# A PSUM bank for the preparation of two recurrences, an earlier place for the second group's start, and a drain that steps only its own heads, in a hybrid decoder layer

## The chip, the core and the metric

The kernel runs on one core of one Trainium2 chip. The metric is the device time of one launch in microseconds (us); it is given as the median of several runs. TensorE (PE) does the matrix multiplications and writes to PSUM, VectorE (DVE) and ScalarE (ACT) do elementwise work, GpSimd (POOL) a few small operations, and SyncE (SP) issues the DMAs that bring in the weights.

## The reference

One decoder layer on x of 256 positions by 2048 channels, all in float32:

```python
x = layer_norm(alpha * x + 0.5 * swiglu(x, ffn1_w_gate, ffn1_w_up, ffn1_w_down), ln1_g, ln1_b)
p = x @ w_in                                     # columns of both mixers
o_attn = diff_attn_group(p[..., :ATTN_COLS], ...)   # 8 heads, two softmaxes each, ALiBi, causal
o_rwkv = rwkv7_group(p[..., ATTN_COLS:], ...)       # 16 heads of 64, delta-rule state over time
mix = jnp.concatenate([o_attn, o_rwkv], axis=-1) @ w_out
x = layer_norm(alpha * x + mix, ln2_g, ln2_b)
x = layer_norm(alpha * x + 0.5 * swiglu(x, ffn2_w_gate, ffn2_w_up, ffn2_w_down), ln3_g, ln3_b)
```

The recurrence of a head carries a 64 by 64 state over the 256 positions, with a decay, a key, a value and a rate for every position:

```python
sa = einsum('bhvk,bhk->bhv', state, -kk_t)
state = state * w_t + sa[..., None] * (kk_t * a_t) + v_t[..., None] * k_t
y_t = einsum('bhvk,bhk->bhv', state, r_t)
```

## The kernel before

**Main stream.** Every large product goes through `Stream.block` (L119). It takes two rows of 128 of the weight matrix at a time by 512 columns: SP loads them into `raw` (three buffers), ACT rounds them to `wh` (L137), DVE takes the rest as `wl` (L138), and PE multiplies three times, high by high, low by high, high by low (L113 to L115). Each step of a block gives 6 such large matmuls for the first 128 positions and 6 for the second 128, the latter two steps behind in the mixer (`LAG`). The mixer has five buffers each for `wh` and `wl`.

**The mixer's side work.** The mixer lies between the two feed-forward parts. Its side work is written as Python generators that are spawned into the stream. After each step, `run_bg` (L154) lets every generator go on by as much as its credit allows (1.6 units a step for the recurrences, 0.5 for the attention heads). A `drain` emits steps until given generators have ended; before the change it goes round all live generators, one step each (L168 to L180). What the generators emit is the order in which the program is recorded; a scheduler then places the instructions of each engine by a timeline of its own, so an instruction may stand some way from where it was recorded.

**What is in a recurrence.** There are two groups of eight recurrent heads, r1 (g = 0) and r2 (g = 1), and two groups of four attention heads, a1 and a2. `rwkv_cols` makes the columns of a group (three blocks of w_in) and spawns `rwkv_group` (L483) and `rwkv_values` (L456). `rwkv_group` has a preparation and a chain. The preparation: rates and decays from two small products (L496, L497, sigmoids at L500, L501), the running sum (L505), the norm of the keys (L519, L520), eight elementwise steps of 128 by 1024 on DVE (L524 to L545), and the products of all pairs within a chunk (L555, masked at L558). Then a triangular system is solved on DVE in 31 steps (L583, L585), the result goes through DRAM and back (L589 to L601, issued by ACT), and two small products complete it (L608, L619), with transposes at L629. The chain goes over four chunks c of 64 positions, each a sequence of PE steps of eight small matmuls with a DVE or ACT step behind each: L642, L650, L658, then L675 and L681 for the output. The tail of a group: centring (L696, L697), squares (L700), L706, Ln and Exp (L707, L709), scale and shift (L711, L714, L716), and the gate (L727, L730, L731). L81 and L82 split the group's output for the product with w_out.

**An attention head** (`attn_heads`, L760) is a chain over all engines too: logits L774, L776, maximum L779, Exp L784, normalisation L786 to L790, transposes L795, product with the values L801 to L803, root mean square L811 to L825, and transposes L829. Two heads of a group go at the same time.

**PSUM.** The eight banks are: three for the large matmuls' `acc`, two with the tag "at" (transposes and attention), and three with the tag "sm" for all small products of the recurrences.

**The order of the mixer** stands at L839 to L890: columns of r1, a1, r2; drain of a1's heads; columns of a2; then the output projection in three parts, for a1 and r1 together (`parts` entry (0, 2)), for a2, and for r2. Each part first drains the generators that make its input (`ready`, L847). So the last part of the projection needs the end of r2's tail, and the part before it needs the end of a2's heads.

Of the kernel before, what the change touches and what calls it, by code (L numbers as in the profile page):

```python
# [12 lines left out]
AF = mybir.ActivationFunctionType  # L13
# [3 lines left out]
P = 128  # L17
D = 2048
S = 256
# [11 lines left out]
LAG = {"ffn": 4, "mix": 2}  # L31
NW = {"ffn": 7, "mix": 5}
NRAW = 3
BANKS = {"tr": ("at", 2), "sm": ("sm", 3), "at": ("at", 2)}
BG = 1.6
AT = 0.5

# [1 line left out]
def build(tc, A, out):  # L39
# [19 lines left out]
    V, SC, G, T = nc.vector, nc.scalar, nc.gpsimd, nc.tensor  # L59
# [29 lines left out]
    class Stream:  # L89
# [75 lines left out]
                        break  # L165
                    c[0] -= cost

        def until(self, ready):  # L168
            idle = 0
            while not ready():  # L170
                assert idle < len(self.bg)
                g = self.bg.pop(0)
                try:
                    idle = idle + 1 if next(g) is None else 0
                    self.bg.append(g)
                except StopIteration:
                    pass

        def drain(self, gens):
            self.until(lambda: not any(g in self.bg for g in gens))  # L180

    stream = Stream()
    KX = [(k, k) for k in range(16)]
# [146 lines left out]
    def mix(mp, pq, C):  # L330
        vB, om = C["vB"], C["om"]

        def bank(tag, shape=(P, NB)):
            return pq.tile(list(shape), F32, tag=BANKS[tag][0], name=nm(tag), bufs=BANKS[tag][1])

        w_in = A["w_in"][0]
        R0 = 3 * AW
        lora = {}
# [73 lines left out]
                self.tl = hp.tile([P, 4, S], F32, tag=HT["T2"], name=nm("tl")) if g == 0 else mp.tile([P, 4, S], F32, tag="tl", name=nm("tl"))  # L412
                self.cum = hp.tile([P, 4, S], F32, tag=HT["T1"], name=nm("cum")) if g == 0 else qq[:, 1]

        def rwkv_cols(g, prev=None):
            gr = Group(g)
            st = {"prev": prev, "group": gr}
            if prev is not None:
                prev["next"] = st
            st["gen"] = rwkv_group(g, st)  # L420
            stream.spawn(st["gen"], BG)

            def done(tt, acc, i):
# [17 lines left out]
            return st  # L441

        def col(i, g, p):
            k = 24 + 8 * i + 4 * g + p
            return vB[:, k:k + 1]
# [10 lines left out]
        def rwkv_values(g, st):  # L456
            prev = st["prev"]
            while "rk" not in st or (prev is not None and "chain" not in prev):
                yield None
            vp, vv, rk = st["group"].vp, st["group"].vv, st["rk"]  # L460
            SV = hp.tile([P, 4, 4, 2, 64], F32, tag="J1", name=nm("SV"))
            st["SV"] = SV
            for p in range(4):
                ps = bank("sm", (P, 4, P))
                for c in range(4):
                    T.transpose(ps[:, c, :], vp[:, p, c * 64:c * 64 + P], ident)
                SC.copy(out=SV[64:128, p, :, 0, :], in_=ps[64:128, :, 0:64])
                SC.copy(out=SV[0:64, p, 0:3, 1, :], in_=ps[0:64, 1:4, 64:128])
                yield 0.3
            ps = bank("sm", (P, 4, P))  # L470
            for p in range(4):
                T.transpose(ps[0:64, p, :], vv[:, p, 192:256], ident)
            SC.copy(out=SV[0:64, :, 3, 1, :], in_=ps[0:64, :, 64:128])
            yield 0.3
            for hf in range(2):
                ps = bank("sm", (P, 2, S))
                for p in range(2):
                    T.matmul(ps[:, p, :], C["bones"], rk[:, 2 * hf + p, :], start=True, stop=True)
                V.tensor_tensor(out=vv[:, 2 * hf:2 * hf + 2, :], in0=ps, in1=vv[:, 2 * hf:2 * hf + 2, :], op=ALU.mult)
                yield 0.6  # L480
            st["values"] = True

        def rwkv_group(g, st):  # L483
            prev, gr = st["prev"], st["group"]
            AR, BK, vv, al, rh, be, ka, av, tl, cum = gr.AR, gr.BK, gr.vv, gr.al, gr.rh, gr.be, gr.ka, gr.av, gr.tl, gr.cum
            wa = cum.rearrange("p a s -> p (a s)")[:, 0:NB]
# [2 lines left out]
            while "tw" not in lora:  # L489
                yield None  # L490
            for hf in range(2):
                pw = bank("sm", (P, 2, S))
                pl = bank("sm", (P, 2, S))
                for i in range(2):
                    c0 = (2 * hf + i) * P
                    T.matmul(pw[:, i, :], wa[0:64, c0:c0 + P], lora["tw"][0:64], start=True, stop=True)  # L496
                    T.matmul(pl[:, i, :], wa[64:128, c0:c0 + P], lora["tw"][64:128], start=True, stop=True)  # L497
                for i in range(2):
                    p = 2 * hf + i
                    SC.activation(out=tl[:, p, :], in_=pw[:, i, :], func=AF.Sigmoid, bias=col(0, g, p))  # L500
                    SC.activation(out=av[:, p], in_=pl[:, i, :].rearrange("p (c t) -> p c t", c=4), func=AF.Sigmoid, bias=col(1, g, p))  # L501
                yield 0.6

            for p in range(4):
                V.tensor_tensor_scan(out=cum[:, p, :], data0=C["smask"], data1=tl[:, p, :], initial=0.0, op0=ALU.mult, op1=ALU.add)  # L505
# [8 lines left out]
                V.tensor_scalar(out=be[:, p], in0=av[:, p], scalar1=-1.0, scalar2=col(3, g, p), op0=ALU.add, op1=ALU.mult)  # L514
            yield 1.0
            for hf in range(2):
                ps = bank("sm", (P, 2, S))
# [30 lines left out]
                yield None  # L548

            for p in range(4):  # L550
                pe = [bank("sm", (P, 4, P)) for e in range(2)]
                for c in range(4):
                    for e in range(2):
                        r = slice(64 * e, 64 * e + 64)
                        T.matmul(pe[e][:, c, :], BK[r, p, c, e:e + 2].rearrange("p a t -> p (a t)"),  # L555
                                 AR[r, p, c].rearrange("p a t -> p (a t)"), start=True, stop=True)
                for e in range(2):
                    V.tensor_tensor(out=Q[:, p, :, e, :], in0=pe[e], in1=C["maskq"][:, None, :].to_broadcast([P, 4, P]), op=ALU.mult)  # L558
                yield 1.2
# [400 lines left out]
```

## Time and profile before

| | |
|---|---|
| three runs | 2024.72, 2017.95, 2019.3 us; median 2019.3 us |
| the profiled execution | 2024.08 us, its span 2022.2 us, clock 0.984 |
| busy in the span | PE 1977.3 us, DVE 1147.5, ACT 883.7, POOL 35.7 |
| the mixer | about 750 to 1290 us of the span |

The profile is that of one execution. Its page gives the busy time of each engine, a chain of work that ended last, and groups of instructions by line. The trace behind it answers by stretches: for a window of time it gives the busy time of each engine and the granted clock of PE (PEclk, 1.00 is full speed); for a wait it gives who waited for whom; and a timeline lists the instructions one by one, with the idle time before each and what ended it in square brackets. A PE busy time says nothing of the rate: at half the clock the same matmuls are busy for twice as long.

### The profile page before, as it was taken

Reading aid. Unit: us, or ns where it says so; the run is one execution under the profiler, and the core shown is the slowest. Engines: PE = TensorE matmul, PEld = TensorE weight load, DVE = VectorE, ACT = ScalarE, POOL = GpSimd, SP = SyncE. Lnnn points to the kernel's source line nnn. Section 1 sums busy time; section 2 is a strip of 40 time slices with the busy share of each in tenths; the row PEclk is TensorE's granted clock in tenths of the full one; section 3 lists DMA queues with packets and bytes.
Section 4 is the critical chain, followed back from the end, with each engine's and each line's share of the span. In section 5 each row is a group of like instructions: output and inputs, shape, how many; then the busy total and the mean of one; then the engine's idle time right before and its main releaser. Section 6 shows DMA issues by size and latency. Waiting matters only on the chain. (4 is left out here: it accounts for less than half of the span.)

```text
span 2022.2 us, 24923 instructions
## 1 busy us (share of the span) xinstructions
PE 1977.3 (98%) x9671; PEld 1623.3 (80%) x9671; DVE 1147.5 (57%) x1419; ACT 883.7 (44%) x1095; POOL 35.7 (2%) x68
## 2 busy tenths in 40 slices
PE   9999999999999999999999988899999999999997
PEld 7888888888888878887777766788888888888886
DVE  5555554445545566775767865755555444555555
ACT  5444433344443335645574443444444334444432
POOL 0200000000000000000000000000000000000000
PEclk9999999999999999999999978999999999999999
DMA  7766666667666656565444624666665666766663
GB/s 243 218 188 195 185 191 209 207 193 229 192 188 188 196 163 196 160 176 163 136 121 141 207 63 154 194 203 187 189 195 185 206 208 198 230 188 189 187 194 129
DMA packets 202009, 373.35 MB, mean 185 GB/s; under 512 B 22827, under 2 KB 24945, under 8 KB 201121
## 3 DMA queue, kind: packets, MB, share of 16 engines
q1 hardware_dynamic: 182928, 350.53, 57.9%
q10 hardware_dynamic: 17440, 14.29, 2.5%
q0 software_dynamic: 1520, 6.93, 1.0%
q8 instruction: 76, 1.25, 0.3%
q14 instruction: 45, 0.36, 0.1%
HBM read 364.10 MB, written 7.60 MB: 184 GB/s over the span
## 5 line engine op out<-in xcount | busy, mean ns | idle before, releaser
L138 DVE TENSOR_TENSOR wl<-raw,wh 128x1024 fp32r<-128x1024 f32 (+1 forms) x665 | 808.0, 1216 | 670.3 <-ACT wh L137 669.3
L137 ACT CAST wh<-raw 128x1024 fp32r<-128x1024 f32 (+1 forms) x665 | 695.4, 1047 | 848.8 <-PE acc L115 733.6
L115 PE MATMUL acc<-wh,xl 128*128 128x512 f32 (+1 forms) x1952 | 741.8, 392 | 0.5 <-DVE xl L82 0.5
L114 PE MATMUL acc<-wl,xh 128*128 128x512 f32 (+1 forms) x1952 | 737.4, 393 | 0.7 <-DVE wl L138 0.7
L113 PE MATMUL acc<-wh,xh 128*128 128x512 f32 (+1 forms) x1952 | 725.5, 392 | 8.5 <-ACT xh L81 5.6
L113 PEld LDWEIGHTS acc<-wh,xh 128*128 128x128 f32 x1952 | 368.9, 189 | 87.5 <-ACT xh L81 7.1
L115 PEld LDWEIGHTS acc<-wh,xl 128*128 128x128 f32 x1952 | 368.9, 189 | 77.2 <-issue 2.0
L114 PEld LDWEIGHTS acc<-wl,xh 128*128 128x128 f32 x1952 | 369.0, 189 | 76.6 <-DVE wl L138 1.8
L115 PE MATMUL acc<-wh,hh 128*128 128x512 f32 x704 | 254.4, 390 | 0.0
L114 PE MATMUL acc<-wl,hh 128*128 128x512 f32 x704 | 253.5, 389 | 0.0
L113 PE MATMUL acc<-wh,hh 128*128 128x512 f32 x704 | 252.8, 389 | 0.0
L114 PEld LDWEIGHTS acc<-wl,hh 128*128 128x128 f32 x704 | 132.2, 188 | 27.6
L113 PEld LDWEIGHTS acc<-wh,hh 128*128 128x128 f32 x704 | 132.1, 188 | 27.4
L115 PEld LDWEIGHTS acc<-wh,hh 128*128 128x128 f32 x704 | 132.2, 188 | 27.3
L243 DVE TENSOR_TENSOR hh<-tr,hh 128x512 fp32r<-128x512 f32 x44 | 30.4, 691 | 64.1 <-ACT hh L242 64.1
L242 ACT CAST hh<-tr 128x512 fp32r<-128x512 f32 x44 | 25.8, 586 | 91.2 <-PE tr L232 91.2
L229 DVE SCALAR_TENSOR_TENSOR h<-sg,acc 128x512 f32<-128x512 f32 x44 | 30.2, 687 | 34.7 <-PE acc L115 34.7
L224 ACT ACTIVATE sg<-acc 128x512 f32<-128x512 f32 x44 | 26.3, 598 | 43.5 <-PE acc L115 43.5
L232 PEld LDWEIGHTS tr<-ident,h 128*128 128x128 f32 x176 | 21.9, 140 | 5.7
L232 PE MATMUL tr<-ident,h 128*128 128x128 f32 x176 | 26.3, 272 | 0.0
L583 DVE TENSOR_TENSOR itmp<-U,Y 64x31 f32<-64x31 f32 (+15 forms) x62 | 20.6, 333 | 4.1 <-DMA U<-dU 2.8
L585 DVE TENSOR_TENSOR Y<-Y,itmp 64x31 f32<-64x31 f32 (+15 forms) x62 | 20.6, 332 | 1.3
(239 smaller groups left out, 753.2 us busy)
## 6 DMA issues: line engine op xcount, KB each, us to landing
raw<-in_ffn_w_up_dram SPq DMA_DIRECT2D x176, 512.0 KB, 3.9
raw<-in_ffn_w_down_dram SPq DMA_DIRECT2D x176, 512.0 KB, 4.3
raw<-in_ffn_w_gate_dram SPq DMA_DIRECT2D x175, 512.0 KB, 3.9
raw<-in_w_in_dram SPq DMA_DIRECT2D x96, 512.0 KB, 3.7
raw<-in_w_out_dram SPq DMA_DIRECT2D x32, 512.0 KB, 4.1
xs<-y ACTq DMA_DIRECT2D x16, 256.0 KB, 3.3
rc<-xs ACTq DMA_DIRECT2D x16, 256.0 KB, 4.4
lng<-in_ln_g_dram POOLq DMA_DIRECT2D x3, 1024.0 KB, 7.8
```

Source lines behind the costliest of these rows:

```text
L113: T.matmul(a, hi, wh[:, j, :w], start=(ki + j == 0), stop=False)
L114: T.matmul(a, hi, wl[:, j, :w], start=False, stop=False)
L115: T.matmul(a, lo, wh[:, j, :w], start=False, stop=(ki + j == last))
L137: SC.copy(out=wh[:, c, :w], in_=raw[:, c, :w])
L138: V.tensor_tensor(out=wl[:, c, :w], in0=raw[:, c, :w], in1=wh[:, c, :w].bitcast(F32), op=ALU.subtract)
L224: SC.activation(out=s, in_=acc, func=AF.Silu)
L229: V.scalar_tensor_tensor(out=h, in0=sg[tt], scalar=0.5, in1=acc, op0=ALU.mult, op1=ALU.mult)
L232: T.transpose(tr[:, i, :], h[:, i * P:(i + 1) * P], ident)
L242: SC.copy(out=hi, in_=tr)
L243: V.tensor_tensor(out=lo, in0=tr, in1=hi.bitcast(F32), op=ALU.subtract)
L583: V.tensor_tensor(out=tv, in0=U[:, 0:j, j:j + 1].to_broadcast([64, j, 32 - j]), in1=Y[:, j:j + 1, j:32].to_broadcast([64, j, 32 - j]), op= ...
L585: V.tensor_tensor(out=Y[:, 0:j, j:32], in0=Y[:, 0:j, j:32], in1=tv, op=ALU.add)
```

## The change

There are three edits, in the mixer alone. No instruction's work changes.

1. PSUM: the tag "sm" has two banks instead of three, and the third gets the tag "pr". The preparation and the values of a group use "pr" (rates, key norms, transposes of the values, bonus products; of the pair products one of each two in every other pair). The rates' two products, which stood in two banks at once, now stand one after the other in the one bank, each with its sigmoids.
2. `rwkv_cols` is split: `rwkv_start` allocates the group's tiles and spawns its generator, `rwkv_cols` makes the columns. The second group is started right behind the first's columns, ahead of a1's.
3. `drain` steps only the generators that it was given; it steps another one only where none of its own can go on.

```diff
-BANKS = {"tr": ("at", 2), "sm": ("sm", 3), "at": ("at", 2)}
+BANKS = {"tr": ("at", 2), "sm": ("sm", 2), "pr": ("pr", 1), "at": ("at", 2)}
...
+        def advance(self, g):
+            try:
+                return next(g) is not None
+            except StopIteration:
+                self.bg.remove(g)
+                return True
 
         def drain(self, gens):
-            self.until(lambda: not any(g in self.bg for g in gens))
+            while any(g in self.bg for g in gens):
+                if not any([self.advance(g) for g in gens if g in self.bg]):
+                    assert any([self.advance(g) for g in self.bg if g not in gens])
...
-        def rwkv_cols(g, prev=None):
+        def rwkv_start(g, prev=None):
...
             for p in range(4):
-                ps = bank("sm", (P, 4, P))
+                ps = bank("pr", (P, 4, P))
                 for c in range(4):
                     T.transpose(ps[:, c, :], vp[:, p, c * 64:c * 64 + P], ident)
...
             for hf in range(2):
-                pw = bank("sm", (P, 2, S))
-                pl = bank("sm", (P, 2, S))
...
+                for k in range(2):
+                    ps = bank("pr", (P, 2, S))
...
             for p in range(4):
-                pe = [bank("sm", (P, 4, P)) for e in range(2)]
+                pe = [bank("sm", (P, 4, P)), bank(("sm", "pr")[p % 2], (P, 4, P))]
...
-        r1 = rwkv_cols(0)
+        r1 = rwkv_start(0)
+        rwkv_cols(0, r1)
+        r2 = rwkv_start(1, r1)
         a1 = attn_cols(0)
-        r2 = rwkv_cols(1, r1)
+        rwkv_cols(1, r2)
         stream.drain(gens(a1))
```

The built programs show what the three edits move. In the pieces below, a line of the mixer in the changed kernel is one higher than the same line before (L609 is L608, L620 is L619, L697 is L696, L707 is L706, L728 is L727). `acc` is a large matmul's output, `wh` and `wl` its weights, `xh` and `xl` its input.

On PE, where the second group's two small products stand that complete its triangular system (L608 writes what becomes PT, L619 uses it). Before (the one large matmul in it is the last that does not need a2's heads):

```order
L608 MATMUL sm_8451<-YT_8447,Q 32x32 x32
L115 MATMUL acc_9640<-wh_9668,xl_9150 128x512
L619 MATMUL sm_8507<-TT_8441,PT_8448 32x32
L629 MATMUL sm_8544<-ident,BK_7242 128x64 x8
L829 MATMUL at_9414<-ident,ot_9319 128x128 x2
L774 MATMUL at_9441<-k_8144,qq 128x128
L774 MATMUL at_9441<-k_8144,qq 128x256
L619 MATMUL sm_8507<-TT_8441,PT_8448 32x32 x31
```

The same place in the changed program:

```order
L609 MATMUL sm_8451<-YT_8447,Q 32x32 x32
L796 MATMUL at_9276<-ident,s_9180 128x128 x3
L113 MATMUL acc_9424<-wh_9462,xh_9137 128x512
...
L115 MATMUL acc_9424<-wh_9528,xl_9146 128x512
L802 MATMUL at_9315<-v_8145,pT_9280 128x128
L620 MATMUL sm_8507<-TT_8441,PT_8448 32x32
L803 MATMUL at_9315<-v_8145,pT_9280 128x128
L804 MATMUL at_9315<-v_8145,pT_9280 128x128
L113 MATMUL acc_9424<-wh_9528,xh_9145 128x512
L620 MATMUL sm_8507<-TT_8441,PT_8448 32x32 x31
L630 MATMUL sm_8544<-ident,BK_6297 128x64 x8
```

One large matmul stood between L608 and the first of L619, and none between it and the others; now 26 stand between the first two, one more before the others, and 57 between those and the stretch without large matmuls that follows. That stretch begins behind the same large matmul in both programs (the 4608th of the whole program), the last that does not need a2's heads. Before, it holds the rest of L619, L629, both heads' logits and the chain's chunks 0 to 2; now it holds chunk 0 from L658 on and chunks 1 to 3, and both heads from L795 on.

On PE, in the second group's tail, between its centring (L696) and the first large matmul that takes its output (`xh_9865`). Before:

```order
L696 MATMUL sm_8890<-BK_7242,bones 128x256 x2
L696 MATMUL sm_8920<-BK_7242,bones 128x256 x2
L115 MATMUL acc_9831<-wh_9846,xl_9697 128x512
L114 MATMUL acc_9838<-wl_9807,xh_9700 128x512
L115 MATMUL acc_9838<-wh_9806,xl_9701 128x512
L706 MATMUL sm_8925<-BK_7242,bones 128x256 x2
L706 MATMUL sm_8929<-BK_7242,bones 128x256 x2
L727 MATMUL sm_8986<-gs_5667,g_1652_8887 128x256 x2
L730 MATMUL sm_8986<-gs_5668,g_1652_8887 128x256 x2
L727 MATMUL sm_9011<-gs_5667,g_1652_8887 128x256 x2
L730 MATMUL sm_9011<-gs_5668,g_1652_8887 128x256 x2
L113 MATMUL acc_9883<-wh_9878,xh_9865 128x512
```

And now:

```order
L697 MATMUL sm_8890<-BK_6297,bones 128x256 x2
L697 MATMUL sm_8920<-BK_6297,bones 128x256 x2
L115 MATMUL acc_9751<-wh_9746,xl_9697 128x512
...
L115 MATMUL acc_9791<-wh_9786,xl_9697 128x512
L707 MATMUL sm_8925<-BK_6297,bones 128x256 x2
L707 MATMUL sm_8929<-BK_6297,bones 128x256 x2
L113 MATMUL acc_9791<-wh_9806,xh_9696 128x512
...
L728 MATMUL sm_8986<-gs_5667,g_1652_8887 128x256 x2
L731 MATMUL sm_8986<-gs_5668,g_1652_8887 128x256 x2
L728 MATMUL sm_9011<-gs_5667,g_1652_8887 128x256 x2
L731 MATMUL sm_9011<-gs_5668,g_1652_8887 128x256 x2
...
L113 MATMUL acc_9883<-wh_9878,xh_9865 128x512
```

Between L696 and L706 there were 3 large matmuls and are now 23; between L706 and L727 none, and now 19; between the last L730 and the first matmul that needs the output none, and now 23.

On DVE, the second group's elementwise preparation (writes to AR and BK) among the weights' casts (`wl`). Before:

```order
L526 TENSOR_TENSOR AR_7241<-AR_7241,tl_7245 128x16x64
L138 TENSOR_TENSOR wl_8741<-raw_8739,wh_8740 128x1024
L531 SCALAR_TENSOR_TENSOR BK_7242<-BK_7242,AR_7241 128x16x64
L367 SCALAR_TENSOR_TENSOR vv_7243<-praw_8116,om,df_8206 128x256
L533 TENSOR_TENSOR BK_7242<-BK_7242,tl_7245 128x16x64
L138 TENSOR_TENSOR wl_8795<-raw_8793,wh_8794 128x1024
L535 TENSOR_TENSOR BK_7242<-BK_7242,tl_7245 64x16x64
L536 TENSOR_TENSOR BK_7242<-BK_7242,tl_7245 64x16x64
L539 COPY PC_7791<-qq 128x16
L540 TENSOR_TENSOR AR_7241<-AR_7241,qq 128x16x63
L545 TENSOR_TENSOR AR_7241<-AR_7241,qq 128x16x64
L138 TENSOR_TENSOR wl_8842<-raw_8840,wh_8841 128x1024
```

And now, from one cast to the next:

```order
L138 TENSOR_TENSOR wl_8275<-raw_8273,wh_8274 128x1024
L823 TENSOR_TENSOR ars_7802<-ars_7802,fl_7801 128x4
L527 TENSOR_TENSOR AR_6296<-AR_6296,tl_6300 128x16x64
L824 TENSOR_TENSOR ars_7802<-ars_7802 128x2
L532 SCALAR_TENSOR_TENSOR BK_6297<-BK_6297,AR_6296 128x16x64
L826 TENSOR_SCALAR ot_7798<-at_7794,ars_7802 128x128 x2
L534 TENSOR_TENSOR BK_6297<-BK_6297,tl_6300 128x16x64
L536 TENSOR_TENSOR BK_6297<-BK_6297,tl_6300 64x16x64
L537 TENSOR_TENSOR BK_6297<-BK_6297,tl_6300 64x16x64
L813 TENSOR_SCALAR ot_7812<-at_7808 128x256
...
L138 TENSOR_TENSOR wl_8310<-raw_8308,wh_8309 128x1024
```

The preparation begins nine casts earlier than it did, five of its eight large steps lie between two casts, and a1's last two heads share the place with it. The weights' DMAs stand on SP in the same order in both programs. ACT has 16 loads of a function table, one more than before.

More of the change, by code (lines that the diff above doesn't have):

```diff
@@ L166, in run_bg @@
                     c[0] -= cost
[L168 to L177, printed above, removed]
+        def advance(self, g):
[4 more added lines that the diff above has]
+                return True
         def drain(self, gens):
-            self.until(lambda: not any(g in self.bg for g in gens))
+            while any(g in self.bg for g in gens):
+                if not any([self.advance(g) for g in gens if g in self.bg]):
+                    assert any([self.advance(g) for g in self.bg if g not in gens])
     stream = Stream()
@@ L421, in rwkv_cols @@
             stream.spawn(st["gen"], BG)
+            return st
+        def rwkv_cols(g, st):
+            gr = st["group"]
             def done(tt, acc, i):
@@ L440, in rwkv_cols @@
                 stream.block(w_in, R0 + i * AW + g * NB, NB, KX, x_lhs, lambda tt, acc, i=i: done(tt, acc, i))
-            return st
         def col(i, g, p):
@@ L469, in rwkv_values @@
                 yield 0.3
-            ps = bank("sm", (P, 4, P))
+            ps = bank("pr", (P, 4, P))
             for p in range(4):
@@ L475, in rwkv_values @@
             for hf in range(2):
-                ps = bank("sm", (P, 2, S))
+                ps = bank("pr", (P, 2, S))
                 for p in range(2):
@@ L491, in rwkv_group @@
             for hf in range(2):
-                pw = bank("sm", (P, 2, S))
-                pl = bank("sm", (P, 2, S))
[L494 to L502, printed above, removed]
+                for k in range(2):
+                    ps = bank("pr", (P, 2, S))
+                    r = slice(64 * k, 64 * k + 64)
+                    for i in range(2):
+                        c0 = (2 * hf + i) * P
+                        T.matmul(ps[:, i, :], wa[r, c0:c0 + P], lora["tw"][r], start=True, stop=True)
+                    for i in range(2):
+                        p = 2 * hf + i
+                        o, x = (tl[:, p, :], ps[:, i, :]) if k == 0 else (av[:, p], ps[:, i, :].rearrange("p (c t) -> p c t", c=4))
+                        SC.activation(out=o, in_=x, func=AF.Sigmoid, bias=col(k, g, p))
+                    yield 0.6
             for p in range(4):
@@ L516, in rwkv_group @@
             for hf in range(2):
-                ps = bank("sm", (P, 2, S))
+                ps = bank("pr", (P, 2, S))
                 for p in range(2):
```

## The prediction

> **What bounds the kernel now.** I read the page first, then PE's waits in the mixer, then the stretches around them with their granted clock.
>
> ```profile
> PE 1977.3 (98%) x9671; PEld 1623.3 (80%) x9671; DVE 1147.5 (57%) x1419; ACT 883.7 (44%) x1095; POOL 35.7 (2%) x68
> ```
>
> PE is busy for 98% of the span. No PE work is removed, so what can be won is only where PE stands still or runs below full clock. PE's waits between 1040 and 1260 us, in order of their sum (us, times, longest):
>
> ```profile
> PE acc L113 <- ACT xh L81: 5.0, 1, 5.0
> PE sm L619 <- issue: 3.2, 1, 3.2
> PE acc L113 <- ACT wh L137: 2.6, 2, 1.8
> PE sm L706 <- ACT BK L700: 2.1, 1, 2.1
> PE at L795 <- DVE s L790: 1.8, 2, 1.4
> ```
>
> They lie in four stretches, which I cut by the timeline. The columns are the stretch, its length, busy us and instructions of PE, PEld, DVE, ACT and POOL, then PE's granted clock and the DMA's share and rate. The first row, a long stretch of the mixer, is for comparison.
>
> ```profile
> 860.00:1050.00 190.00, 190.00 (x1268) 152.54 (x1267) 131.63 (x264) 105.29 (x193) 5.01 (x5) 1.00 0.53 150
> 1057.30:1076.00 18.70, 16.89 (x73) 13.45 (x74) 18.64 (x22) 8.83 (x10) 0.00 (x0) 0.82 0.45 142
> 1162.90:1178.70 15.80, 12.63 (x198) 10.25 (x197) 11.62 (x23) 9.00 (x16) 1.91 (x1) 0.68 0.54 172
> 1178.70:1200.70 22.00, 17.27 (x231) 14.40 (x230) 15.13 (x54) 9.60 (x38) 2.12 (x2) 0.71 0.01 2
> 1226.30:1246.30 20.00, 12.84 (x38) 9.39 (x38) 9.02 (x15) 9.07 (x10) 0.00 (x0) 0.74 0.31 117
> ```
>
> I call a stretch's work its busy time times the clock, and the rest its excess: idle time and lost clock together. P (from 1057): work 16.89 x 0.82 = 13.8, excess 4.9. A (from 1163): 12.63 x 0.68 = 8.6, excess 7.2. B (from 1179): 17.27 x 0.71 = 12.3, excess 9.7. C (from 1226): 12.84 x 0.74 = 9.5, excess 10.5. Together 32.3 us: that is all that this change can reach.
>
> **A: the second group's small products.** The timeline there, by start and duration:
>
> ```profile
> 1162.91 1.20 PE L608 MATMUL sm<-YT,Q 32*32 32x32 f32 x64
> 1164.04 0.49 PE L115 MATMUL acc<-wh,xl 128*128 128x512 f32 x1
> 1167.70 0.28 PE L619 MATMUL sm<-TT,PT 32*32 32x32 f32 x2 [3.17 <-issue]
> 1170.26 0.58 ACT L610 COPY PT<-sm 32x512 f32<-32x512 f32 x1
> 1171.15 1.06 PE L619 MATMUL sm<-TT,PT 32*32 32x32 f32 x32
> 1206.20 0.39 PE L114 MATMUL acc<-wl,xh 128*128 128x512 f32 x1
> 1206.43 0.40 PE L115 MATMUL acc<-wh,xl 128*128 128x512 f32 x1
> ```
>
> L619 needs L608's result by way of a copy on ACT: 1170.84 - 1164.11 = 6.7 us from the end of L608 to the end of the copy, and PE has one large matmul for it. At full clock a large matmul takes 0.23 us (the last two rows). The change puts 26 of them there, 26 x 0.23 = 6.0 us, and six small products of the heads besides. I take that as cover for all of the 6.7 us but some tenths. A's 8.6 us of work goes among large matmuls; its excess should fall from 7.2 to about 0.7: **-6.5** (bounds -4 and -7.2). Moving r2's chain ahead also moves the DMAs behind which ACT waits (L597, L601) into the large matmuls. The first group had just that, between 860 and 1050 us where PE never idled:
>
> ```profile
> ACT wh L137 <- DMA YT<-dYT: 7.3, 1, 7.3
> ```
>
> So I take nothing for it.
>
> **B: the stretch without large matmuls.** It ends when a2's last head is split:
>
> ```profile
> 1177.83 0.92 PE L774 MATMUL at<-k,qq 64*128 64x128 f32 x4
> 1183.03 0.48 PE L658 MATMUL sm<-SV,BT 128*64 128x64 f32 x2 [1.14 <-DVE SV L651]
> 1191.61 0.34 PE L658 MATMUL sm<-SV,BT 128*64 128x64 f32 x4
> 1198.12 1.14 ACT L81 CAST xh<-qq 128x512 fp32r<-128x512 f32 x2 [0.21 <-DVE qq L830]
> 1200.73 0.79 PE L113 MATMUL acc<-wh,xh 128*128 128x512 f32 x1
> 1217.61 0.68 PE L675 MATMUL sm<-Q,SV 128*64 128x64 f32 x14
> 1218.21 0.68 PE L681 MATMUL sm<-AR,St 64*64 64x64 f32 x16
> ```
>
> From the last head's logits (end 1178.75) to the first large matmul behind them it takes 22.0 us. In the changed program the same logits stand three large matmuls ahead of the stretch, so this chain stays bare. Chunk 3 joins it, with L650 of chunk 3 ahead of the last head's transposes, while chunk 0's first half leaves. Before, chunk 0's L658 began 4.3 us into the stretch; now it is among the first. A chunk took 8.6 us (1183.03 to 1191.61). So the recurrence gains 4.3 us and is given up to 8.6 more: the stretch becomes anything from 20 to 26 us; I take 22.5, since PE now enters it at full clock. The work in it grows by three steps of eight small matmuls at 0.60 us (1217.61 to 1218.21): 12.3 + 1.8 = 14.1. Excess 22.5 - 14.1 = 8.4: **-1.3** (bounds -4 and +2).
>
> **C: the second group's tail.**
>
> ```profile
> 1228.45 3.34 PE L706 MATMUL sm<-BK,bones 128*128 128x256 f32 x8 [2.14 <-ACT BK L700]
> 1230.17 1.28 ACT L707 ACT_TABLE_LOAD   x1 [1.77 <-PE sm L706]
> 1231.59 1.41 PE L727 MATMUL sm<-gs,g 128*128 128x256 f32 x4
> 1235.04 1.12 PE L730 MATMUL sm<-gs,g 32*128 32x256 f32 x4
> 1241.19 0.79 PE L113 MATMUL acc<-wh,xh 128*128 128x512 f32 x1 [5.03 <-ACT xh L81]
> L138 DVE TENSOR_TENSOR wl<-raw,wh 128x1024 fp32r<-128x1024 f32 x11 | 13.5, 1224 | 13.8 <-ACT wh L137 13.7
> L874 DVE TENSOR_TENSOR y<-y,acc 128x512 f32<-128x512 f32 x12 | 8.1, 682 | 4.5 <-PE acc L115 4.5
> ```
>
> From the start of L706 to the first matmul that needs the output the chain takes 1241.19 - 1228.45 = 12.7 us, and PE had only its own part of it to do. Ahead of L706 23 large matmuls (5.3 us) now hide the wait of 2.1 us. Behind it the chain gets longer: on DVE two casts and two sums (L874) now stand between L711 and L731, 2 x 1.22 + 2 x 0.68 = 3.8 us; at full clock L706's first half is 0.8 us shorter: 15.7 us. The cover is L706 at full clock (1.7), 19 large matmuls (4.4), L727 and L730 (1231.59 to 1236.16 at half clock, so 2.3) and 23 large matmuls (5.3): 13.7 us. A wait of 2.0 us is left, with about 1 us of clock lost behind it. Excess 3.0 instead of 10.5: **-7.5** (bounds -2 and -10.5).
>
> **P: casts behind the second group's preparation.**
>
> ```profile
> 1067.17 0.50 PE L113 MATMUL acc<-wh,xh 128*128 128x512 f32 x1 [1.76 <-ACT wh L137]
> 1070.00:1075.00 5.00, 5.00 (x14) 3.81 (x14) 5.00 (x9) 2.06 (x2) 0.00 (x0) 0.50 0.83 299
> L526 DVE TENSOR_TENSOR AR<-AR,tl 128x1024 f32<-128x1024 f32 x1 | 1.2, 1225 | 1.2 <-ACT tl L523 1.2
> L545 DVE TENSOR_TENSOR AR<-AR,qq 128x1024 f32<-128x1024 f32 x1 | 1.2, 1221 | 0.0
> ```
>
> Steps of 1.22 us each, from L526 to L545, hold DVE; the longest run of them without a cast was L535 to L545, 3 x 1.22 + 1.20 + 0.18 = 5.0 us. The weights fell behind, PE waited, and the clock was at half afterwards. In the changed program the run is five large steps, 6.1 us, plus the heads' small ones, some 1.5 us, but it stands where PE has the chain's and the heads' small products to do between large ones, so that it uses up weights more slowly. I cannot tell which prevails and take half of the excess: **-2.4** (bounds -4.9 and +4).
>
> **Smaller terms.** The order holds 143 runs of large matmuls on PE, 133 before. A change from large to small begins with a gap:
>
> ```profile
> 1217.60 0.54 PEld L675 LDWEIGHTS sm<-Q,SV 128*64 128x64 f32 x14 [0.36 <-issue]
> ```
>
> Ten more of them cost between 0 and 10 x 0.36 = 3.6 us; gaps of that kind go from A, so I take **+1.5**. One more table load on ACT (1.28 us in C's row) costs 0, since ACT is busy 44% of the time; on PE's path it would be +1.3. [...] The split of the rates and the new drain cost nothing of their own: they change places, not work.
>
> **The sum**: -6.5 - 1.3 - 7.5 - 2.4 + 1.5 = -16.2 us. The profiled execution took 2024.1 us (span 2022.2), 4.8 above the median of the three runs, 2019.3. I apply the difference to the median: 2019.3 - 16.2 = **2003.1 us**.
>
> **The rivals.**
>
> *The clock stays full* (chance 0.12). In B no single wait before was over 1.4 us (L795's, in the list of waits), and the half clock there was carried over from A's wait of 3.2 us. If PE enters B at full clock and keeps it, B takes 20 us with 14.1 of work (2.5 less than I took), the wait of 2.0 us in C costs no clock (-1), and P's lost clock, 16.89 x 0.18 = 3.0 us, is gone rather than halved (-1.5): 5 us less, 1998.1 us. Against it: behind P's wait of 1.76 us the clock was 0.50 for 5 us and more. [...]
>
> *The tail stays bare* (chance 0.15). The sums on DVE wait for PE's accumulators, and PE may not get ahead of them; then 23 large matmuls run out early, PE waits some 7 us again, and C gives only 2 us: 2008.6 us. For it speaks that DVE takes its work in order, with 3.8 us of other work inside the chain.
>
> *DVE starves PE at the second group's preparation* (chance 0.12). With the run of 7.6 us where it was 5.0, the wait of 1.76 grows by 2.6 to 4.4 us, with as much half clock again: P's excess is 8.7 instead of 4.9. P then costs 3.8 instead of giving 2.4: 2009.3 us. Against it speaks the first group's preparation, with four steps of the kind in a row and PE busy throughout:
>
> ```profile
> 820.00:840.00 20.00, 20.00 (x91) 16.27 (x90) 15.11 (x16) 14.15 (x16) 0.00 (x0) 1.00 0.40 118
> ```
>
> *Slower: one bank for the preparation holds PE up* (chance 0.05). The bank is used 30 times (16 for rates, key norms and bonus, 10 for the values, 4 for pair products), each time to be emptied by ACT or DVE before PE, which works in order, may write again:
>
> ```profile
> L467 ACT COPY SV<-sm 64x256 f32<-64x256 f32 x4 | 1.5, 368 | 3.5 <-PE sm L466 3.5
> ```
>
> Copies of some 0.7 us, behind a cast of about 1.05 us, are 1.8 us. Each wait of 1.05 us on PE makes 30 x 1.05 = 31 us: 2035 us. It decides from 16.2 / 30 = 0.54 us a use on. Against it: the order leaves 21 to 25 large matmuls, about 5 us, between nearly all uses.
>
> **How the numbers follow.** The forecast has a chance of 0.56. Its own bounds and the rivals at 1998 and 2009 give the range: all four stretches at their best give 2019.3 - 26.6 = 1992.7, less 3 for the scatter of three runs, 1990; both losing rivals together give 2014.8, so 2014 above. A measurement of this kernel can tell about 0.3%, 6 us, from no change, which puts the bounds at 2013.2 and 2025.4. Faster: the forecast, the full clock and most of the two middle rivals, 0.86. Within: what is left of those, 0.09. Slower: the bank, 0.05.
>
> **What would show it.** Right: no wait on L619; PE's waits before L706 gone; the first matmul that needs the second group's output waits 1 to 3 us instead of 5; the stretch without large matmuls lasts 21 to 24 us instead of 38 (A and B together), still with a lowered clock. Wrong: waits of PE on small products named pr; a wait on ACT wh of over 4 us at the preparation; a mixer that ends less than 8 us earlier.

## The result, and the profile after

| | before | changed |
|---|---|---|
| median, compared runs | 2020.41 us (4 runs, 2017.95 to 2024.72) | 2008.57 us (4 runs, 2007.99 to 2008.85) |
| the profiled execution | 2024.08 us, span 2022.2 | 2008.56 us, span 2006.8 |
| granted clock, whole span | 0.984 | 0.990 |

The ratio is 0.9941, 95% interval 0.9927 to 0.9955: the change makes the kernel 11.8 us faster by the medians, and 15.5 us by the two profiled executions. The forecast was 2003.1 us. PE's waits over the whole changed kernel (us, times, longest; the 0.2 on L113 and 0.6 of the first row's 4.0 lie ahead of the mixer):

```profile
...
PE tr L75 <- DVE y L194: 4.0, 2, 3.4
PE acc L114 <- DVE wl L138: 3.9, 3, 2.2
PE at L75 <- DVE y L194: 3.0, 1, 3.0
PE sm L643 <- DVE SV L668: 2.0, 2, 1.5
PE sm L651 <- DVE Rs L645: 1.6, 2, 0.9
...
PE acc L113 <- ACT xh L81: 0.2, 1, 0.2
```

The waits of 3.2 us on L619, 2.1 us before L706 and 5.0 us on the second group's output are gone. New is a wait of 2.2 us on a weight cast. No wait falls on a product named pr. For an account by stages I take the excess, as the prediction does (length less PE busy times clock). Stretches of before (columns as in the prediction):

```profile
840.00:860.00 20.00, 19.61 (x119) 15.81 (x119) 16.60 (x27) 12.02 (x17) 0.00 (x0) 1.00 0.69 196
1040.00:1080.00 40.00, 37.43 (x179) 30.16 (x178) 33.08 (x44) 24.90 (x31) 0.00 (x0) 0.91 0.50 153
1140.00:1220.00 80.00, 72.10 (x665) 58.25 (x664) 52.53 (x131) 33.36 (x84) 6.16 (x6) 0.85 0.38 113
1220.00:1260.00 40.00, 32.84 (x126) 25.68 (x125) 22.30 (x30) 14.35 (x15) 0.53 (x1) 0.87 0.45 153
1260.00:1300.00 40.00, 34.84 (x152) 26.92 (x151) 33.54 (x48) 15.26 (x19) 2.01 (x2) 0.91 0.61 183
```

The stretches of the changed kernel that answer to them, its second group's preparation being 30 us earlier and its layer norm 15 us:

```profile
840.00:860.00 20.00, 18.86 (x105) 15.23 (x104) 18.35 (x26) 9.93 (x14) 0.00 (x0) 1.00 0.63 192
1020.00:1040.00 20.00, 17.83 (x102) 14.15 (x102) 14.70 (x27) 12.96 (x26) 2.02 (x2) 0.91 0.34 99
1140.00:1220.00 80.00, 74.20 (x691) 59.54 (x690) 49.52 (x120) 42.12 (x99) 5.27 (x6) 0.91 0.47 149
1220.00:1240.00 20.00, 20.00 (x87) 15.68 (x86) 18.39 (x26) 7.82 (x9) 0.00 (x0) 1.00 0.50 158
1240.00:1280.00 40.00, 36.17 (x156) 28.82 (x155) 36.27 (x51) 14.51 (x18) 2.00 (x2) 0.87 0.56 174
```

| excess, us | before | changed | difference | forecast |
|---|---|---|---|---|
| first group's preparation (840) | 0.4 | 1.1 | +0.7 | 0 |
| P, second group's preparation | 5.9 | 3.8 | -2.1 | -2.4 |
| A and B (1140 to 1220) | 18.7 | 12.5 | -6.2 | -7.8 |
| C, the tail | 11.4 | 0.0 | -11.4 | -7.5 |
| layer norm | 8.3 | 8.5 | +0.2 | 0 |
| sum | | | -18.8 | -17.7 |
| the rest, by the spans (-15.4) | | | +3.4 | +1.5 |

The rest is what no stretch has as excess, and so PE work: busy time at full clock is some 3 us longer. The changed order has ten more changes from large to small products; whether they are the cause is taken up below. In the tail of the changed kernel PE runs at 1.00 without a gap from 1205 to 1250 us; its small products there:

```profile
1213.48 1.89 PE L707 MATMUL sm<-BK,bones 128*128 128x256 f32 x8
...
1219.54 1.03 PE L728 MATMUL sm<-gs,g 128*128 128x256 f32 x4
...
1222.61 1.12 PE L731 MATMUL sm<-gs,g 32*128 32x256 f32 x4
```

And the end of the chain on ACT, the split that gives the second group's output:

```profile
1228.10 1.14 ACT L81 CAST xh<-og 128x512 fp32r<-128x512 f32 x2
```

From L707's start to the end of the split are 1229.24 - 1213.48 = 15.8 us, the 15.7 us that the prediction worked out. PE comes to the first matmul that takes it, 23 large ones behind L731, at 1229.0: it had 15.6 us of work, not 13.7. The chain is just covered.

### The profile page after: what moved, and what is told of

Same layout as the page of the kernel before. It is cut to its first block, busy times and chain, and to the rows that moved or that the text cites. A ratio compares the mean times of both kernels' runs of the same rounds, so it can differ in the third digit from the quotient of the medians.

```text
span 2006.8 us, 24924 instructions
## 1 busy us (share of the span) xinstructions
PE 1972.1 (98%) x9671; PEld 1618.6 (81%) x9671; DVE 1145.7 (57%) x1419; ACT 885.0 (44%) x1096; POOL 34.2 (2%) x68
## 4 chain that ended last, share of the span: by engine, by line
PE 91%; DVE 4%; DMA 2%; ACT 1%; issue 1%; ACTq 0%; POOL 0%; DVEq 0%
PE acc L113 28%; PE acc L115 28%; PE acc L114 28%; DVE wl L138 1%; DMA raw<-in_ffn_w_gate_dram 1%; PE tr L230 1%; ACT wh L137 1%; DVE y L193 1%; DVE y L194 1%; PE sm L556 0%; PE tr L353 0%; DMA raw<-in_ffn_w_up_dram 0%; PE pr L498 0%; PE at L775 0%; PE tr L75 0%
## 5 line engine op out<-in xcount | busy, mean ns | idle before, releaser
L138 DVE TENSOR_TENSOR wl<-raw,wh 128x1024 fp32r<-128x1024 f32 (+1 forms) x665 | 807.9, 1217 | 649.1 <-ACT wh L137 648.4
L113 PE MATMUL acc<-wh,xh 128*128 128x512 f32 (+1 forms) x1952 | 728.1, 392 | 0.3 <-ACT xh L81 0.2
L113 PEld LDWEIGHTS acc<-wh,xh 128*128 128x128 f32 x1952 | 368.2, 189 | 79.1 <-issue 3.0
L113 PE MATMUL acc<-wh,hh 128*128 128x512 f32 x704 | 252.6, 389 | 0.0
L113 PEld LDWEIGHTS acc<-wh,hh 128*128 128x128 f32 x704 | 132.1, 188 | 27.4
```

Of the source, the lines that this page charges most:

```text
L113: T.matmul(a, hi, wh[:, j, :w], start=(ki + j == 0), stop=False)
L138: V.tensor_tensor(out=wl[:, c, :w], in0=raw[:, c, :w], in1=wh[:, c, :w].bitcast(F32), op=ALU.subtract)
```

## The experiments

The theory was that the gain comes from the place that the second group's chain and tail get among large matmuls. Rivals: the bank brings it, or the drain. Second questions were what makes the new wait on the cast, and what the half clock owes to the waits.

**1. The bank edit alone** (before, with the hunks of the diff on banks and rates):

```diff
-BANKS = {"tr": ("at", 2), "sm": ("sm", 3), "at": ("at", 2)}
+BANKS = {"tr": ("at", 2), "sm": ("sm", 2), "pr": ("pr", 1), "at": ("at", 2)}
```

> The kernel before with the PSUM edit alone (sm two banks, pr one, the rates' products one after the other); the second group starts where it did, the drain is the old one. Theory (place): the gain comes from where the second group's chain and tail stand among large matmuls, whichever edit puts them there. In this program 27 large matmuls stand between L608 and L619, so the wait of 3.2 us on L619 goes (-6.5); but only 18 stand behind L706 and none behind L727, so in the tail a chain of 15.7 us meets 1.7 + 18 x 0.23 + 4.2 = 10.0 us of cover: PE still waits 5 to 6 us at the first matmul that takes the second group's output, and the tail gives only -2 to -4. Together 2010 to 2014 us, about half of what all edits give. Rival (bank): the bank is what frees the second group, and this program is as fast as the changed kernel, 2007 to 2010.

Measured: 2009.88 us beside 2018.65 of before, ratio 0.9963 (0.9950 to 0.9976). Its wait on L619 is gone, and its tail has the uncovered chain (PE, by start and duration):

```profile
1214.74 1.89 PE L706 MATMUL sm<-BK,bones 128*128 128x256 f32 x8
...
1223.64 1.13 PE L730 MATMUL sm<-gs,g 32*128 32x256 f32 x4
1230.03 0.79 PE L113 MATMUL acc<-wh,xh 128*128 128x512 f32 x1 [5.26 <-ACT xh L81]
```

The time lies where the two expectations meet, at the top of the rival's range and 0.1 us under the theory's, and does not tell them apart; the ratio is some 0.2% above the changed kernel's 0.9941 and 0.9949 (run 9), and the intervals overlap. The trace does: the wait of 5.26 us is the expected 5 to 6, so counting the large matmuls behind L706 foretells it. Alone, the bank gives about two thirds of the change's gain. Part of that neither expectation had: P's excess, 5.9 us before, is gone here.

```profile
1020.00:1080.00 60.00, 60.00 (x336) 48.98 (x334) 43.04 (x68) 31.47 (x43) 1.98 (x1) 1.00 0.53 158
```

**2. The early start alone** (before, with `rwkv_cols` split and the new order of calls):

```diff
-        r1 = rwkv_cols(0)
+        r1 = rwkv_start(0)
+        rwkv_cols(0, r1)
+        r2 = rwkv_start(1, r1)
         a1 = attn_cols(0)
-        r2 = rwkv_cols(1, r1)
+        rwkv_cols(1, r2)
```

> The kernel before with the early start of the second group alone; three sm banks for everything, the old drain. Theory (place): 25 large matmuls stand between L608 and L619, 42 behind L706 with 31 of them behind the last L727, so both waits go (-6.5 and about -10); the last head's logits stand directly at the stretch without large matmuls, which costs up to 3 us there. Together 2005 to 2010 us, as fast as the changed kernel or faster. Rival (bank): without a bank of its own the preparation waits for the chain's banks and PE for it; 2018 to 2022, as before.

Measured: 1998.78 us, ratio 0.9913 (0.9899 to 0.9927). This is faster than the changed kernel, and also faster than I expected: the rival is out, and the bank, laid on top of the early start, costs time. Its waits on L619 and on the second group's output are gone too.

**3. The drain alone** (before, with `advance` and the new `drain`).

> The kernel before with the new drain alone. Theory: the same instructions stand in the same order on all five engines as before, so nothing changes: within 0.2% of the kernel before, which also shows what two equal programs differ by. Rival (the drain carries a share of the gain): 4 us or more faster.

Measured: 2019.2 us beside 2018.65, ratio 1.0008 (0.9998 to 1.0019). The built program explains it: every instruction, with its waits, stands where it stood, on all five engines. In the changed kernel nothing is left to order at a drain: when a1 is drained none of its heads is live, and when a2 is drained both its generators stand at their last `yield`. With the old drain put back, the changed kernel too has the same order on all engines. So the third edit does nothing. As a second execution of the old order, its profile is worth a look; two of the stretches above:

```profile
1140.00:1220.00 80.00, 73.41 (x678) 58.96 (x677) 52.13 (x127) 33.98 (x84) 6.69 (x6) 0.87 0.42 126
1220.00:1260.00 40.00, 31.66 (x130) 24.92 (x129) 25.56 (x34) 15.40 (x16) 0.00 (x0) 0.91 0.41 141
```

Its span is 2016.3 us, 5.9 less than that of the profile I argued from. A and B have 16.1 us of excess there instead of 18.7; C is as it was (11.2).

**4. One of the DVE steps on POOL** (changed kernel, second group):

```diff
-            V.tensor_tensor(out=merge(be[0:64]), in0=merge(av[0:64]), in1=merge(v4(tl)[0:64]), op=ALU.mult)
+            (G if g == 1 else V).tensor_tensor(out=merge(be[0:64]), in0=merge(av[0:64]), in1=merge(v4(tl)[0:64]), op=ALU.mult)
```

> The changed kernel, where for the second group one of the five large elementwise steps that stand on DVE between two casts (L536) is computed by POOL. Theory (DVE holds back the casts): PE's wait of 2.2 us on a weight cast near 1033 us shrinks by the step's 1.22 us, to 0.9 to 1.2 us, and the lowered clock behind it (0.90 and 0.76 in two slices of 5 us) becomes nearly full: 2 to 3 us won between 1020 and 1045 us. Elsewhere its order differs: L727 stands directly ahead of the large matmuls that take the second group's output, 18 large matmuls behind L706, so the tail loses 4 to 6 us; in all 2009 to 2013. Rival (the casts were late for another reason, such as the loads of the weights): the wait near 1033 us stays at 2 us or more.

Measured: 2014.89 us beside 2018.65, ratio 0.9982 (0.9973 to 0.9992), worse than expected. First the changed kernel's DVE there: two casts (L138), and between them five large steps, of which the fourth is the one that is moved; the last row is PE's wait on the second cast:

```profile
1022.70 1.23 DVE L138 TENSOR_TENSOR wl<-raw,wh 128x1024 fp32r<-128x1024 f32 x1 [0.48 <-ACT wh L137]
...
1029.12 1.21 DVE L536 TENSOR_TENSOR BK<-BK,tl 64x1024 f32<-64x1024 f32 x1
...
1032.21 1.22 DVE L138 TENSOR_TENSOR wl<-raw,wh 128x1024 fp32r<-128x1024 f32 x1
...
1033.48 0.50 PE L114 MATMUL acc<-wl,xh 128*128 128x512 f32 x1 [2.17 <-DVE wl L138]
```

Then POOL, DVE and PE of this run:

```profile
1022.93 1.23 DVE L138 TENSOR_TENSOR wl<-raw,wh 128x1024 fp32r<-128x1024 f32 x1 [0.48 <-ACT wh L137]
...
1028.29 3.39 POOL L536 TENSOR_TENSOR BK<-BK,tl 64x1024 f32<-64x1024 f32 x1 [5.04 <-ACT ot L812]
...
1029.47 3.29 DVE L537 TENSOR_TENSOR BK<-BK,tl 64x1024 f32<-64x1024 f32 x1
...
1033.40 1.22 DVE L138 TENSOR_TENSOR wl<-raw,wh 128x1024 fp32r<-128x1024 f32 x1
...
1034.67 0.50 PE L114 MATMUL acc<-wl,xh 128*128 128x512 f32 x1 [3.14 <-DVE wl L138]
```

While POOL worked, DVE's next step took 3.29 us instead of 1.22. It ended 1.1 us behind POOL's step (1029.47 + 3.29 against 1028.29 + 3.39), so the rows fit a DVE step that stood until POOL was done and then ran at its usual pace; one pair of steps does not show more. From cast to cast it is now 10.5 us where it was 9.5, and PE's wait is 3.14 where it was 2.17: a microsecond for a microsecond. The relief became an addition. By its letter the rival's sign came true (a wait of 2 us or more), but not its reason: DVE works without a gap up to the cast, so it is DVE's run and not a late load that holds the cast back. The clock stayed full behind this wait:

```profile
1020.00:1040.00 20.00, 16.86 (x104) 13.51 (x104) 16.02 (x29) 13.28 (x26) 5.42 (x3) 1.00 0.30 89
```

**5. A longer tail** (changed kernel, ahead of L717):

```diff
+            if g == 1:
+                for _ in range(2):
+                    V.tensor_tensor(out=sq, in0=Yc, in1=Yc, op=ALU.add)
```

> The changed kernel, where the second group's tail gets two more DVE steps of 128 by 1024 ahead of L717 (each 1.22 us; their result is overwritten). Every PE instruction stands where it stood. Theory (the tail is just covered, with nothing to spare): in the changed kernel the chain from L707 to the split of the second group's output took 15.8 us and the work that PE had meanwhile 15.7, so each further us of chain is a us of PE's wait: the first matmul that takes the output waits 2.2 to 2.7 us instead of 0.2, with some half clock behind it; 2011 to 2013 us. Rival (the cover is ample): no wait, 2008 to 2009.

Measured: 2014.17 us beside 2020.82, ratio 0.9967 (0.9954 to 0.9980), above the expected 2011 to 2013. The first matmul that takes the second group's output:

```profile
1227.34 0.79 PE L113 MATMUL acc<-wh,xh 128*128 128x512 f32 x1 [3.63 <-ACT xh L81]
```

A wait of 3.6 us where there was none, and where 2.2 to 2.7 were expected: the two steps took 2.47 us on DVE, and another sum and cast, 1.7 us, now came in ahead of the gate's product. The tail has nothing to spare.

**6 and 10. The changed kernel without a bank of its own** (one program, run twice; the rates stay one after the other):

```diff
-BANKS = {"tr": ("at", 2), "sm": ("sm", 2), "pr": ("pr", 1), "at": ("at", 2)}
+BANKS = {"tr": ("at", 2), "sm": ("sm", 3), "pr": ("sm", 3), "at": ("at", 2)}
```

> The early start with the rates' two products one after the other, but with three sm banks for everything: the changed kernel without the bank of its own. From there on it has the order of the run with the early start alone. Theory (the separate bank is what costs the 10 us between the early start alone and all three edits, by moving the preparation's DVE steps and the chain): as fast as the early start alone, 1997 to 2001 us. Rival (the serial rates cost it): 2005 or more.

Measured: 1999.34 us beside 2020.82, ratio 0.9901 (0.9885 to 0.9918), as the early start alone.

> The changed kernel without the bank of its own (three sm banks for everything), on the same chip as the changed kernel. Theory (the bank costs, given the early start): 7 to 10 us faster than the changed kernel beside it. Rival (the difference of the earlier runs was one of chips): within 3 us of it.

Measured, on one chip with run 9, the changed kernel: 1999.92 us against 2008.04; ratios to before 0.9912 (0.9894 to 0.9929) and 0.9949 (0.9933 to 0.9965). The bank of its own costs 8 us. Where, shows the profile of run 10:

```profile
1020.00:1060.00 40.00, 39.53 (x186) 32.38 (x186) 30.28 (x43) 28.62 (x38) 1.01 (x1) 1.00 0.40 118
1140.00:1220.00 80.00, 74.97 (x706) 59.44 (x705) 53.68 (x125) 40.25 (x92) 5.34 (x6) 0.98 0.45 139
```

P has 0.5 us of excess instead of 3.8, A and B 6.5 instead of 12.5. Run 9's profile, on the same chip, has 3.8 and 10.8, so that the two places make 7.6 us of the 8.0 between the two spans. In P the five steps now come 20 us later, the first of them with casts between (DVE):

```profile
1045.52 1.23 DVE L527 TENSOR_TENSOR AR<-AR,tl 128x1024 f32<-128x1024 f32 x1 [0.90 <-ACT tl L524]
1047.06 1.22 DVE L138 TENSOR_TENSOR wl<-raw,wh 128x1024 fp32r<-128x1024 f32 x1
1048.19 1.22 DVE L532 SCALAR_TENSOR_TENSOR BK<-BK,AR 128x1024 f32<-128x1024 f32 x1
```

In A and B the waits of PE add up to 3.5 us (1155 to 1203 us), against 4.9 in the changed kernel, and the clock over 1140 to 1220 us is 0.98 instead of 0.91. That the bank moves these places is shown. Why two banks and one make just this order was not taken further. The wait at P takes both edits: run 1, with the bank, has none there, and run 10, with the early start, 0.5 us.

**7. Two banks for all small products** (run 2 with):

```diff
-BANKS = {"tr": ("at", 2), "sm": ("sm", 3), "at": ("at", 2)}
+BANKS = {"tr": ("at", 3), "sm": ("sm", 2), "at": ("at", 3)}
```

> The early start with only two sm banks, shared by preparation and chain; the third bank goes to the tag at (transposes and attention). Theory (banks count through the place that the second group's chain gets): with two banks for all small products its chain falls back, L608 and L619 stand at the stretch without large matmuls again, the last chunk and the whole tail behind the last large matmul that does not need it; the wait behind L608 is back (+7) and the tail of 16 us with chunk 3 and the centring ahead of it stands bare (12 to 18 us more than now): slower than the kernel before, 2022 to 2035 us. Rival (a third bank for the heads shortens the stretch that ends with them, and the chain's place is of little weight): 1998 to 2010.

Measured: 2024.15 us beside 2020.82, ratio 1.0019 (1.0008 to 1.0030). PE in its tail:

```profile
1229.14 3.11 PE L709 MATMUL sm<-BK,bones 128*128 128x256 f32 x8 [1.93 <-ACT BK L703]
...
1241.65 0.80 PE L113 MATMUL acc<-wh,xh 128*128 128x512 f32 x1 [4.40 <-ACT xh L81]
```

The tail is bare again, waits of 1.9 and 4.4 us with it. The wait behind L608 that I expected did not come back (0.3 us on the product that stands for L619). At the other end a wait came that I had not foreseen, 8.0 us ahead of the transposes of a2's heads (L798, for DVE's normalisation). It is a little slower than before, and some 25 us slower than run 6 on the same chip: with two banks for all small products the early start wins nothing. How much of that is the tail and how much the heads, with their third bank, this run does not separate.

**8. One DVE step left out** (changed kernel, second group; without the step its output is not the reference's):

```diff
-            V.tensor_tensor(out=merge(av[64:128]), in0=merge(av[64:128]), in1=merge(v4(tl)[64:128]), op=ALU.mult)
+            if g == 0:
+                V.tensor_tensor(out=merge(av[64:128]), in0=merge(av[64:128]), in1=merge(v4(tl)[64:128]), op=ALU.mult)
```

> The changed kernel, in which the second group leaves out one of the large DVE steps between two casts (L537, half of the rates' product with the decay), so its output is not the reference's. Theory (DVE's run of steps holds back the cast, us for us): PE's wait near 1033 us falls from 2.2 to about 1.0 us, and the clock stays full there, 2 to 2.5 us of excess less in 1020 to 1045 us. The tail has 18 large matmuls behind L706 and none behind L727, as in the runs with the bank alone and with one step on POOL, so PE waits 5 to 6 us at the second group's output; in all 2008 to 2012 us. Rival: the wait near 1033 us stays at 2 us.

Measured: 2011.67 us, ratio 0.9958 (0.9943 to 0.9972). PE near the cast, and the stretch:

```profile
1031.99 0.50 PE L114 MATMUL acc<-wl,xh 128*128 128x512 f32 x1 [0.69 <-DVE wl L138]
```

```profile
1020.00:1040.00 20.00, 19.31 (x115) 15.58 (x115) 16.02 (x31) 14.22 (x27) 2.03 (x2) 1.00 0.34 99
```

The step took 1.22 us and the wait fell by 1.48, from 2.17 to 0.69. With run 4 this settles it: the length of DVE's run between two casts makes the wait. The tail waits 5.3 us here, as in run 1.

**9. The changed kernel once more.**

> The changed kernel once more, on the same chip as the next run, for a second profiled execution. Theory (the waits belong to the program, the half clock behind them to the execution): the wait of 2.2 us near 1033 us, those of 1.5 and 0.9 to 1.2 us at the start of the stretch without large matmuls and the covered tail are all there again to 0.3 us, while the clock behind them differs, so that the excess at 1020 to 1040 us is anything from 2.2 to 3.8 us and the stretch lasts 23 to 26 us; 2007 to 2011 us. Rival (the clock follows the waits): the same clock in the same slices as in the first profile, 0.90 and 0.76 at 1030 to 1040, 0.58, 0.50 and 0.55 at 1180 to 1195.

Measured: 2008.04 us beside 2017.8. The three waits came again to 0.1 us (2.2, 1.5 and 0.9). The clock did not follow them: 1030 to 1040 and 1190 to 1195 us in the changed kernel's first profile,

```profile
1030.00:1035.00 5.00, 2.83 (x13) 2.08 (x12) 4.92 (x9) 2.39 (x7) 0.00 (x0) 0.90 0.12 10
1035.00:1040.00 5.00, 5.00 (x20) 3.97 (x19) 3.12 (x8) 1.65 (x2) 1.01 (x1) 0.76 0.63 203
1190.00:1195.00 5.00, 5.00 (x52) 4.20 (x53) 1.31 (x5) 1.62 (x8) 0.00 (x0) 0.55 0.01 2
```

in this run,

```profile
1030.00:1035.00 5.00, 2.83 (x13) 2.14 (x12) 4.92 (x9) 2.58 (x7) 0.00 (x0) 0.92 0.07 7
1035.00:1040.00 5.00, 5.00 (x19) 3.94 (x19) 3.12 (x8) 1.46 (x2) 1.01 (x1) 0.74 0.66 202
...
1190.00:1195.00 5.00, 4.81 (x75) 4.05 (x74) 1.58 (x6) 2.36 (x13) 0.00 (x0) 0.88 0.01 2
```

and in run 5, which has the same PE order up to its tail:

```profile
1030.00:1035.00 5.00, 2.91 (x14) 2.38 (x15) 4.94 (x10) 1.65 (x6) 0.00 (x0) 1.00 0.33 95
1035.00:1040.00 5.00, 5.00 (x24) 4.14 (x23) 4.38 (x11) 3.08 (x4) 1.01 (x1) 1.00 0.62 168
1190.00:1195.00 5.00, 3.38 (x67) 2.59 (x62) 4.85 (x24) 1.77 (x10) 2.12 (x2) 1.00 0.01 3
```

At the cast run 9 does not exclude the rival (0.92 and 0.74 beside 0.90 and 0.76), but run 5 does: the same wait of 2.2 us, and the clock at 1.00. In the stretch without large matmuls all three differ, and it lasts 25.6, 24.1 and 23.2 us.

## Why the prediction was right or wrong

The direction and the main reason held: the change wins by putting the second group's chain and tail among large matmuls. By its steps:

- **A, -6.5: held.** The wait on L619 is gone and L609 to L630 run at full clock (1.00 from 1140 to 1170 us).
- **B, -1.3: the length was too small.** It was to last 22.5 us and lasted 25.6 (24.1 and 23.2 in two more executions). That the clock would be lowered was right, that PE enters at full clock too (1.00 from 1175 to 1180 us); I did not allow for a clock that would stay near half for 15 us (0.50 to 0.58 in the slices from 1180 to 1195 us). PE's longest wait in it, 1.5 us on L643, comes from DVE, which had a cast and the heads' steps ahead of L668 (changed kernel, DVE):

```profile
1177.03 1.22 DVE L138 TENSOR_TENSOR wl<-raw,wh 128x1024 fp32r<-128x1024 f32 x1
...
1179.16 1.01 DVE L780 TENSOR_REDUCE mx<-s 128x2 f32<-128x256 f32 x2
1180.08 0.86 DVE L668 TENSOR_TENSOR SV<-sm,PC 64x256 f32<-64x256 f32 x2
```

  Before, the half clock in B was not carried over from A's wait, as the rival of a full clock has it: the clock was back at 1.00 from 1178 to 1181 us, and at 0.50 from 1182 to 1191. A and B together gave 6.2 us instead of 7.8. One pair of profiles cannot settle that size: with the excess of runs 9 and 5 in the same stretch, 10.8 and 9.1 us, the gain is 7.9 and 9.6, and from run 3's 16.1 it is 3.6.
- **C, -7.5: the cover was mis-sized.** The chain took 15.8 us, as worked out (15.7). The cover was 15.6 instead of 13.7, because L728 and L731 take 4.2 us at full clock: the 4.6 us of before were taken for half clock and halved. The rows could have told: L730 took 1.12 us before, as L731 does now. So no wait was left, where one of 1 to 3 us was named as the sign of being right, and C gave all 11.4. The rival of a bare tail is out, though by no margin: run 5 shows each added step as a wait.
- **P, -2.4: right in size by luck, wrong in kind.** Half the excess was taken because I could not tell which way it would go. The old wait is gone altogether; the run of five steps that I had named made a new one of 2.2 us, 30 us earlier, with 3.8 us of excess. The rival (DVE starves PE at the preparation) named the mechanism and put too high a price on it. What I did not see is 0.7 us of the same at the first group's preparation.
- **The changes from large to small, +1.5: too low.** The work grew by about 3 us, and the ten changes are its likely cause. Busy time times clock, added up over the whole span in windows of 10 us, is 1954.9 and 1954.0 us for the old order (before, run 3), 1951.9 for run 7 with four such changes fewer, 1956.8 and 1957.3 for runs 1 and 2 with six and eight more, 1958.3 and 1959.6 for the changed kernel (the result's profile and run 9). That is some 0.4 us a change, but no run varies the changes alone.
- **The bank, costing nothing:** no wait falls on its products, so the rival of PE held up there did not come about. But it has a price in another way: it moves the preparation and the chain, and with the early start it costs 8 us (run 10). I weighed the three edits as one and never asked what each does to the order. The drain was said to change places; it changes none (run 3).
- **The basis.** Against the profiled execution the forecast was -16.2 and the measurement -15.5: applied there, it would have said 2007.9 us, where 2008.6 was measured. I took it from the median, 4.8 us under that execution, and that is most of the gap of 5.5 us. Part of the 4.8 was the very excess that I counted as won: run 3, the same order, has 2.6 us less of it in A and B.
- **The sum.** That -16.2 came so near to the profiles' -15.5 is partly luck: C gave 3.9 us more than forecast, A and B 1.6 less, and the work grew by 1.9 more.

The best version found is the early start without the bank, with the rates one after the other or not: 1998.8 to 1999.9 us in three comparisons, ratios 0.9901 to 0.9913.

## What to carry to other kernels

Time each edit of a bundle alone, and compare the built orders first: here one edit did nothing, one made the kernel fast, and one took back 8 us of it while looking like a gain by itself. Whether a dependent chain is covered can be counted before running, from its length and the large matmuls that stand beside it; take the durations of the cover from a place at full clock. A gain that is lost clock in one profile should be held against a second execution before it is subtracted from a median.

## What the runs showed of the hardware

- The lowered clock behind a wait was no fixed price in these runs. With 2.2 us of wait at the same matmul the clock over 1035 to 1040 us was 0.76 in the changed kernel's first profile, 0.74 in run 9 and 1.00 in run 5; the wait of 3.14 us in run 4 cost no clock either (1.00 from 1030 to 1050 us). Runs 4, 5 and 9 were on different chips, but one chip shows a spread too: 21 runs of the kernel before, beside runs 1 to 4, took 2014.8 to 2023.2 us, with a clock over the whole span of 0.990 in the shortest and 0.985 in the longest. What decides whether the clock falls behind such a wait, no run here shows.
- A POOL step of 64 by 1024 beside a DVE step of the same kind (run 4): DVE's took 3.29 us instead of 1.22 and ended 1.1 us behind POOL's, which took 3.39.
